# A two-layer decoder trunk: early work on one token half, y's sums moved into layer 0, and another first order in layer 1

## The chip, the core and the metric

The kernel runs on one core of a Trainium2 chip. The metric is the device time of one execution in microseconds. Five engines are spoken of: PE (matrix products), DVE and POOL (elementwise), ACT (activations and copies), SP (which issues DMAs). Each runs its own instructions in a fixed order, set when the program is built; an instruction waits at the head of its queue until its inputs and its buffer are ready.

## The reference

The input x is 1024 tokens by 1024 channels, float32. Two layers follow, each `h = h + mixer(rms_norm(h))`, and a last RMSNorm.

```python
def pooling_mixer(u, w_in, w_group, scale, w_out):        # layer 0
    xb, z = jnp.split(u @ w_in, 2, axis=-1)               # 2048 channels each
    pooled = trailing mean over 2/4/8/16 tokens (4 channel groups) minus self
    mixed = per group of 512 channels: pooled @ w_group[g]
    y = mixed * scale * silu(z)
    return y @ w_out                                      # 2048 -> 1024

def stick_breaking_mixer(u, w_in, w_out):                 # layer 1
    q, k, v, z = split(u @ w_in)                          # 16 heads
    o = stick_breaking_attention(q, k, v)
    return (o * silu(z)) @ w_out
```

## The kernel before, in words

**Products.** A float32 tile is split into a rounded part and a remainder (`split`, lines 92 to 99: a copy on ACT, L97, a subtraction on DVE, L98). `mm3` (lines 86 to 90) makes one product of three matmuls from two split tiles: L88, L89, L90. A tile is 128 x 512.

**Seven products instead of eight.** Layer 0's input projection and output projection use Strassen's scheme in Winograd's form: the operands are cut into 2 x 2 blocks, and seven products of sums of blocks give the four result blocks. For the input projection the blocks of u are named B[j, l, kb]: j is the half of the channels, l the half of the tokens (l = 0 is the later half in memory, `HALVES = (1, 0)`), kb one of four tiles. The operands of the seven products are G[1] to G[7]: G1 and G2 are blocks of the first token half, G3 a block of the second, G4 to G7 sums of blocks of both (`u_sums`, lines 183 to 193).

**Opening** (lines 299 to 314). `load_x(l)` loads eight tiles of x's transpose, squares each on ACT and sums the squares over channels by matmuls against ones (L156), then makes the RMS factor (POOL, L162), spreads it by four transposes (L165) and copies it (L167). `to_u` scales a tile (L173) and splits it into a G. A `Group` is two blocks of 128 output columns; groups at 0 and 2 give xb, those at 16 and 18 z, for the first pooling group. `first` is the product with G1, `second` the one with G2, both into PSUM bank p1; `rest` makes the other five with the weights' sums, which POOL adds (lines 231 to 234 and 257), and DVE combines them. Two groups, `x0` and `x1`, do `first` and `second` on the first token half before the second half is loaded and `u_sums` runs.

**Layer 0's loop** (lines 316 to 332). For each of four pooling groups `gi`: two xb groups, pooling of their four blocks (`pool_block`, DVE), two z groups with SiLU, and for each of four blocks `mixed` (lines 286 to 297): 24 matmuls, the scaling by z on DVE (L295) in the tile t0, and one write of t0, 512 KB, to `y_dram` (L297). There are two buffers for t0, seven for raw weights (`a_raw`).

**Output projection** (lines 347 to 485). Seven products of eight steps each: the first is `ops1`, then `ops6`, one with Y[1, 0], `ops7`, `ops4`, one with S1 and `ops3`. Each step loads weight blocks (`wload`) and, in `ops1` and `ops6`, the four blocks of y (`load_y`, L356). POOL makes the sums of y (L404 to L406, L434) and those of the weights (L410, L411, L430, L470). The x tiles are loaded again and the results added. `to_u1(l)` (lines 449 to 465) makes layer 1's input for a token half: RMS factor, scaling, transposes on PE (L460), split by ACT and DVE (L464, L465). `to_u1(0)` comes before `ops3`, `to_u1(1)` after it.

**Layer 1** (lines 488 to 813). Work comes in items for q and k, z, v and the output projection of a head. PSUM's eight banks go from the pool `banks` to four pools with 3, 2, 2 and 1 banks. `head0` (line 735) is the list of items made before the first scores.

**What sets the order.** The tile framework schedules the instructions of each engine with its own simulation, mostly by program order among those that it takes to be ready; so queues don't follow the text line by line. Tiles of a pool rotate over its buffers, and pools opened later lie in the space of those closed before.

Of the kernel before, what the change touches and what calls it, by code (L numbers as in the profile page):

```python
# [15 lines left out]
P = 128  # L16
# [29 lines left out]
def trunk(ctx, tc, x, xt, g, pw, pg, psc, pwo, sqk, sv, sz, swo, nf, out):  # L46
# [36 lines left out]
    y_dram = dram.tile([DI // P, P, S], F32, name="y_dram")  # L83
# [47 lines left out]
    with tc.tile_pool(name="l0", bufs=2) as l0:  # L131
# [10 lines left out]

        def load_x(l, then={}):
# [22 lines left out]
            rsb = l0.tile([P, 512], F32, name="rsb", bufs=2)  # L166
# [3 lines left out]
        def to_u(k, l, n, rsb):  # L170
# [12 lines left out]
        def u_sums(kb):  # L183
            b11, b21, b12, b22 = B[0, 0, kb], B[1, 0, kb], B[0, 1, kb], B[1, 1, kb]
            t3 = l0.tile([P, 512], F32, name="w_raw", bufs=3)
            nc.vector.tensor_tensor(t3, b22, b12, ALU.subtract)
            u_split(7, kb, t3)
            nc.gpsimd.tensor_tensor(b12, b11, b12, ALU.subtract)
            nc.vector.tensor_tensor(b11, t3, b11, ALU.add)
            u_split(6, kb, b11)  # L190
            u_split(5, kb, b12)
            nc.gpsimd.tensor_tensor(b11, b11, b21, ALU.subtract)
            u_split(4, kb, b11)
# [6 lines left out]
        def tmp():  # L200
            return l0.tile([P, 512], F32, name="avx", bufs=4)

        class Group:


            def __init__(self, c):
                self.c, self.a11, self.a12 = c, None, None

            def load(self):
                self.a11 = raw_of(pw[self.c][:, :512], l0, "a_raw", bufs=7)  # L210

            def first(self):

                if self.a11 is None:
                    self.load()
                self.p1 = bank()
                product(self.p1, split(self.a11), 1)
                self.a1 = tmp()
                act(self.a1, self.p1, AF.Copy)

            def second(self):
                self.a12 = raw_of(pw[self.c][:, 512:], l0, "a_raw", bufs=7)
                product(self.p1, split(self.a12), 2, True)

            def rest(self, dst, fn):

                a11, c = self.a11, self.c
                a21 = raw_of(pw[c + 1][:, :512], l0, "a_raw", bufs=7)
                a22 = raw_of(pw[c + 1][:, 512:], l0, "a_raw", bufs=7)
# [17 lines left out]
                v = tmp()  # L247
                nc.vector.tensor_tensor(v, p6, self.a1, ALU.subtract)
# [5 lines left out]
                if self.a12 is None:  # L254
                    self.second()
                out(0, 0, self.p1, None)
                add(self.a12, self.a12, a11, ALU.add)
                product(p7, split(a22), 4, True)
                out(1, 0, v, p7)
                product(p5, split(self.a12), 3, True)  # L260
# [25 lines left out]
        def mixed(gi, o, pooled, t0):  # L286
# [10 lines left out]
            nc.sync.dma_start(y_dram[kb], t0)  # L297

        x0, x1 = Group(0), Group(2)
        rsb = load_x(0, {1: x0.load, 3: x1.load})  # L300
        for k in range(4):
            to_u(k, 0, 1, rsb)
        x0.first()
        x1.first()
        for k in range(4, 8):
            to_u(k, 0, 2, rsb)
        x0.second()
        x1.second()
        rsb = load_x(1)
        for kb in range(4):  # L310
            to_u(kb, 1, 0, rsb)
            to_u(4 + kb, 1, 3, rsb)
            u_sums(kb)
        nc.sync.dma_start(sc_sb, psc)

        for gi in range(len(WINDOWS)):
            pooled = {}
            for cp in (0, 2):
                grp = (x0 if cp == 0 else x1) if gi == 0 else Group(gi * 4 + cp)
                if gi:  # L320
                    grp.first()
                dst = [xb_tile() for _ in range(2)]
                grp.rest(dst, AF.Copy)
                for i in range(2):
                    pool_block(gi, cp + i, dst[i], pooled)
            for op in (0, 2):
                grp = Group(16 + gi * 4 + op)
                grp.first()
                dst = [l0.tile([P, S], F32, name="t0") for _ in range(2)]
                grp.rest(dst, AF.Silu)  # L330
                for i in range(2):
                    mixed(gi, op + i, pooled, dst[i])
# [14 lines left out]
    with tc.tile_pool(name="ob", bufs=4, reuse_waits="tile") as ob:  # L347
# [3 lines left out]
        Y, T3, S1, S2 = {}, {}, {}, {}  # L351

        def load_y(j, l, kb):
            half = HALVES[l]
            Y[j, l, kb] = slot()
            nc.sync.dma_start(Y[j, l, kb], y_dram[8 * j + kb][:, half * 512:half * 512 + 512])  # L356

        def out_product(ps, operands, more=False, by_tile=None):

            ops = [None] * 8  # L360

            def step(t, kb):
                (wh, wl), (yh, yl) = ops[kb]
                ts_ = slice(t * P, (t + 1) * P)
                mm3(ps[t], yh[:, ts_], yl[:, ts_], wh, wl, kb == 0 and not more, kb == 7, more)

            for kb in range(8):
                ops[kb] = operands(kb)
                for t in range(4):
                    step(t, kb)  # L370
# [17 lines left out]
        def ops1(kb):  # L388
            load_y(0, 0, kb)
# [465 lines left out]
```

## Time and profile before

| | us |
|---|---|
| median of 3 runs (1659.06 to 1661.23) | 1659.06 |
| the profiled execution | 1659.5 |
| its span | 1657.7 |
| PE busy in the span | 1565.2 (94%) |
| DVE busy | 1110.8 (67%) |
| ACT busy | 672.6 (41%) |
| POOL busy | 383.7 (23%) |

The span is the time from the first to the last instruction of the profiled execution; all positions below count from its start. A matmul's end is modelled, so PE's busy time holds overlaps; the distance of two starts is the better price. "Idle" in brackets behind an instruction is what its engine waited just before it, and for whom.

### The profile page before, as it was taken

How to read it: one execution, taken by the hardware profiler on the slowest of the kernel's cores; microseconds unless marked ns; L12 is line 12 of the kernel's file. 1: busy time of each engine (PE TensorE's matmuls, PEld its weight loads, DVE VectorE, ACT ScalarE, POOL GpSimd, SP SyncE). 2: the span in 40 equal slices, each digit the busy share in tenths (PEclk: the TensorE clock that was granted, in tenths of full speed). 3: DMA queues.
4: the chain of work that ended last, by engine and by line, in shares of the span. 5: the costliest groups of instructions: out<-in, count | busy, mean ns of one | idle time of the engine just before them, and what ended most of it. 6: DMA issues, size and time to landing. Idle time of an engine off the chain costs nothing.

```text
span 1657.7 us, 23250 instructions
## 1 busy us (share of the span) xinstructions
PE 1565.2 (94%) x8360; PEld 1349.1 (81%) x8360; DVE 1110.8 (67%) x1643; ACT 672.6 (41%) x1328; POOL 383.7 (23%) x822
## 2 busy tenths in 40 slices
PE   7399999999985999799999999999999999999997
PEld 7278888888863788698988988988988988988986
DVE  3785674957842788457685675676667667657678
ACT  5334232323321445445344434434435435335344
POOL 0542222223029552111111101102102102101113
PEclk9599999999997999899999999999999999999999
DMA  4021221222167450112012011111011011021012
GB/s 146 0 88 67 89 83 70 64 83 64 38 231 264 148 168 3 57 44 59 14 51 65 29 43 57 39 47 49 33 52 52 26 58 45 26 64 39 27 43 104
DMA packets 59955, 113.20 MB, mean 68 GB/s; under 512 B 7360, under 2 KB 7360, under 8 KB 59840
## 3 DMA queue, kind: packets, MB, share of 16 engines
q1 hardware_dynamic: 59696, 111.71, 20.9%
q8 instruction: 66, 1.08, 0.3%
q14 instruction: 49, 0.40, 0.1%
q10 hardware_dynamic: 144, 0.01, 0.0%
HBM read 90.72 MB, written 12.58 MB: 62 GB/s over the span
## 4 chain that ended last, share of the span: by engine, by line
PE 89%; DVE 3%; POOL 3%; DMA 2%; issue 1%; SPq 1%; ACT 1%; POOLq 0%; DVEq 0%; ACTq 0%
PE pd L88 14%; PE pd L90 14%; PE pd L89 14%; PE bk L88 10%; PE bk L89 10%; PE bk L90 10%; PE pt L686 4%; PE po L88 2%; PE po L89 2%; PE po L90 2%; PE pq L642 2%; PE pq L643 2%; DMA slot<-y_dram 2%; PE bk L156 1%; POOL slot L405 0%
## 5 line engine op out<-in xcount | busy, mean ns | idle before, releaser
L654 DVE TENSOR_TENSOR_SCAN om<-om 128x257 f32<-128x257 f32 (+1 forms) x192 | 187.3, 979 | 85.9 <-POOL om L651 34.7
L88 PE MATMUL pd<-slot,w_hi 128*128 128x512 f32 x512 | 202.2, 395 | 8.4 <-DVE slot L465 8.4
L89 PE MATMUL pd<-slot,w_hi 128*128 128x512 f32 x512 | 201.9, 394 | 0.0
L90 PE MATMUL pd<-slot,w_lo 128*128 128x512 f32 x512 | 200.3, 392 | 0.0
L98 DVE TENSOR_TENSOR w_lo<-w_raw,w_hi 128x512 fp32r<-128x512 f32 x192 | 143.4, 756 | 68.6 <-ACT w_hi L97 66.6
L97 ACT ACTIVATE w_hi<-w_raw 128x512 fp32r<-128x512 f32 x192 | 120.0, 630 | 139.9 <-PE pd L89 67.4
L647 ACT ACTIVATE om<-pq 128x256 f32<-128x256 f32 (+1 forms) x192 | 94.4, 492 | 180.1 <-PE pq L643 173.6
L88 PE MATMUL pd<-w_hi,slot 128*128 128x256 f32 x512 | 146.4, 286 | 0.0
L90 PE MATMUL pd<-w_hi,slot 128*128 128x256 f32 x512 | 144.7, 283 | 0.0
L89 PE MATMUL pd<-w_lo,slot 128*128 128x256 f32 x512 | 144.3, 282 | 0.0
L651 POOL TENSOR_SCALAR_AFFINE_SELECT om<-om 128x128 f32<-128x128 f32 x128 | 49.1, 385 | 375.8 <-ACT om L647 373.2
L97 ACT ACTIVATE w_hi<-a_raw 128x512 fp32r<-128x512 f32 x96 | 59.8, 629 | 154.7 <-PE bk L89 108.1
L88 PE MATMUL bk<-w_hi,y_hi 128*128 128x512 f32 x224 | 92.3, 418 | 30.5 <-ACT y_hi L97 22.3
L88 PEld LDWEIGHTS pd<-slot,w_hi 128*128 128x128 f32 x512 | 96.8, 189 | 27.0 <-DVE slot L465 8.7
L690 DVE TENSOR_TENSOR at_l<-pt,at_h 128x512 fp32r<-128x512 f32 (+1 forms) x160 | 99.5, 625 | 20.2 <-ACT at_h L689 20.0
L90 PEld LDWEIGHTS pd<-slot,w_lo 128*128 128x128 f32 x512 | 96.6, 189 | 19.6
L89 PEld LDWEIGHTS pd<-slot,w_hi 128*128 128x128 f32 x512 | 96.6, 189 | 18.7
L689 ACT ACTIVATE at_h<-pt 128x512 fp32r<-128x512 f32 (+1 forms) x160 | 86.6, 552 | 60.5 <-PE pt L686 59.8
L658 DVE TENSOR_TENSOR om<-pq,om 128x256 f32<-128x256 f32 (+1 forms) x192 | 105.0, 551 | 9.2 <-ACT v_h L576 0.5
L88 PE MATMUL pd<-w_hi,y_h 128*128 128x512 f32 x256 | 107.0, 418 | 0.4 <-ACT y_h L715 0.4
L89 PE MATMUL pd<-w_lo,y_h 128*128 128x512 f32 x256 | 102.2, 399 | 0.0
L90 PE MATMUL pd<-w_hi,y_l 128*128 128x512 f32 x256 | 100.3, 395 | 0.0
(182 smaller groups left out, 4031.5 us busy)
## 6 DMA issues: line engine op xcount, KB each, us to landing
w_raw<-in_pwo SPq DMA_DIRECT2D x72, 256.0 KB, 3.9
a_raw<-in_pw SPq DMA_DIRECT2D x64, 256.0 KB, 2.8
y_dram<-t SPq DMA_DIRECT2D x16, 512.0 KB, 2.6
slot<-y_dram SPq DMA_DIRECT2D x32, 256.0 KB, 5.5
w_raw<-in_sqk SPq DMA_DIRECT2D x32, 256.0 KB, 2.8
w_raw<-in_sz SPq DMA_DIRECT2D x32, 256.0 KB, 3.0
w_raw<-in_sv SPq DMA_DIRECT2D x32, 256.0 KB, 2.7
w_raw<-in_swo SPq DMA_DIRECT2D x32, 256.0 KB, 2.6
```

Source lines behind the costliest of these rows:

```text
L88: nc.tensor.matmul(ps, lhsT=lh, rhs=rh, start=start, stop=False, skip_group_check=more)
L89: nc.tensor.matmul(ps, lhsT=lh, rhs=rl, start=False, stop=False, skip_group_check=more)
L90: nc.tensor.matmul(ps, lhsT=ll, rhs=rh, start=False, stop=stop, skip_group_check=more)
L97: act(hi, raw, AF.Copy)
L98: nc.vector.tensor_tensor(lo, raw, hi, ALU.subtract)
L647: act(om[:, 1:1 + n], pz, AF.Sigmoid, scale=-ZSCALE)
L651: nc.gpsimd.affine_select(out=om[:, 1:1 + P], in_=om[:, 1:1 + P], pattern=[[1, P]], base=0, channel_multiplier=-1, compare_op=ALU.is_gt, f ...
L654: nc.vector.tensor_tensor_scan(out=om[:, :1 + n], data0=om[:, :1 + n], data1=om[:, :1 + n], initial=1.0 if s.first else carry[r], op0=ALU. ...
L658: nc.vector.tensor_tensor(om[:, :n], pz, om[:, :n], ALU.mult)
L686: nc.tensor.transpose(tp[:, c * P:(c + 1) * P], om[:, (j - b0) * P:(j - b0 + 1) * P], ident)
L689: act(ah[:, :n], tp[:, :n], AF.Copy)
L690: nc.vector.tensor_tensor(al[:, :n], tp[:, :n], ah[:, :n], ALU.subtract)
```

## The change

The change has four parts. (1) Four groups (two xb, two z) do `first` and `second` on the first token half; they read their a11 and a12 weights again in `rest`. `load_x(1)` adds squares pairwise on POOL before the sum by matmul. `u_sums` scales the second half itself and orders its work by product: G7's and G6's sums first, then the splits of 6, 7, 5, 4, 3. (2) `mixed` makes y's sums on POOL as soon as a block of y is there and writes each of the seven operands to an array of its own in HBM; for the last eight blocks it reads back the matching first two (`old`, one buffer). (3) The output projection loads one y operand per step, and its own y sums are gone. (4) `head0` begins with the later token half of q and z and that half's v; the items for the other half load and split their weights again. Buffers: a_raw 6 instead of 7, avx 5 instead of 4, the RMS factor uses w_raw.

```diff
-    y_dram = dram.tile([DI // P, P, S], F32, name="y_dram")
+    yd = {n: dram.tile([8, P, 512], F32, name=f"y{n}_dram") for n in range(8)}
...
+        def wide(i):
+            return l0.tile([P, S + 16], F32, name="xb" if i % 2 else "wsum")
...
+            def ssq(sq, first, last):
+                for j in range(4):
+                    nc.tensor.matmul(
+                        ps[:, 2 * j:2 * j + 2], lhsT=sq[:, j * P:(j + 1) * P], rhs=ones,
+                        start=first and j == 0, stop=last, skip_group_check=True)
...
-                sq = l0.tile([P, S + 16], F32, name="xb" if k % 2 else "wsum")[:, :512]
+                sq = wide(k)[:, :512]
                 act(sq, t, AF.Square)
-                for j in range(4):
-                    nc.tensor.matmul(
-                        ps[:, 2 * j:2 * j + 2], lhsT=sq[:, j * P:(j + 1) * P], rhs=ones,
-                        start=k == 0 and j == 0, stop=k == NK - 1, skip_group_check=True)
+                if l == 0:
+                    ssq(sq, k == 0, k == NK - 1)
+                elif k % 2:
+                    nc.gpsimd.tensor_tensor(sq, sq, before, ALU.add)
+                    ssq(sq, k == 1, k == NK - 1)
+                before = sq
...
+        def u_sums(rsb):
+            t3 = []
+            for kb in range(4):
+                b11, b12, b22 = B[0, 0, kb], B[0, 1, kb], B[1, 1, kb]
+                to_u(kb, 1, rsb)
+                to_u(4 + kb, 1, rsb)
+                t3.append(wide(kb)[:, :512])
+                nc.vector.tensor_tensor(t3[kb], b22, b12, ALU.subtract)
+                nc.gpsimd.tensor_tensor(b12, b11, b12, ALU.subtract)
+                if kb:
+                    t2(kb - 1, t3)
+            t2(3, t3)
+            for kb in range(4):
+                u_split(7, kb, t3[kb])
+            for kb in range(4):
+                u_split(5, kb, B[0, 1, kb])
+            for kb in range(4):
+                nc.gpsimd.tensor_tensor(B[0, 0, kb], B[0, 0, kb], B[1, 0, kb], ALU.subtract)
+                u_split(4, kb, B[0, 0, kb])
+            for kb in range(4):
+                u_split(3, kb, B[1, 1, kb])
+
+        def t2(kb, t3):
+            nc.vector.tensor_tensor(B[0, 0, kb], t3[kb], B[0, 0, kb], ALU.add)
+            u_split(6, kb, B[0, 0, kb])
...
+            def load(self, i, j):
+                self.a[i, j] = raw_of(pw[self.c + i][:, j * 512:j * 512 + 512], l0, "a_raw", bufs=6)
...
+            def ahead(self):
+                self.second()
+                self.a, self.early = {}, True
...
             def rest(self, dst, fn):
+                if self.early:
+                    self.load(0, 0)
+                else:
+                    self.first()
+                self.load(1, 0)
+                self.load(1, 1)
...
-            nc.sync.dma_start(y_dram[kb], t0)
+            b = t0[:, 512:], t0[:, :512]
+            j, kb = divmod(kb, 8)
+            sub = nc.gpsimd.tensor_tensor
+            def put(n, t):
+                nc.sync.dma_start(yd[n][kb], t)
+            put((1, 2)[j], b[0])
+            put((0, 3)[j], b[1])
+            if j == 0:
+                sub(b[1], b[0], b[1], ALU.subtract)
+                put(5, b[1])
+            else:
+                o = l0.tile([P, S], F32, name="old", bufs=1)
+                for n in range(2):
+                    nc.sync.dma_start(o[:, n * 512:n * 512 + 512], yd[n][kb])
+                b12, b11 = o[:, :512], o[:, 512:]
+                sub(b12, b[1], b12, ALU.subtract)
+                put(7, b12)
+                sub(b11, b12, b11, ALU.add)
+                put(6, b11)
+                sub(b[0], b11, b[0], ALU.subtract)
+                put(4, b[0])
...
+        early = xs + zs
+        rsb = load_x(0, {2 * i + 1: lambda i=i: early[i].load(0, 0) for i in range(4)})
         for k in range(4):
-            to_u(k, 0, 1, rsb)
-        x0.first()
-        x1.first()
+            to_u(k, 0, rsb, 1)
+        for grp in early:
+            grp.first()
         for k in range(4, 8):
-            to_u(k, 0, 2, rsb)
-        x0.second()
-        x1.second()
-        rsb = load_x(1)
-        for kb in range(4):
-            to_u(kb, 1, 0, rsb)
-            to_u(4 + kb, 1, 3, rsb)
-            u_sums(kb)
+            to_u(k, 0, rsb, 2)
+        for grp in early:
+            grp.ahead()
+        u_sums(load_x(1))
...
+        def ysplit(n, kb):
+            return split(raw_of(yd[n][kb], ob, "y_raw"), ob, "y")
...
         def ops6(kb):
-            for jl in ((0, 1), (1, 1), (1, 0)):
-                load_y(*jl, kb)
-            T3[kb] = slot()
-            add(T3[kb], Y[1, 1, kb], Y[0, 1, kb], ALU.subtract)
-            add(Y[0, 1, kb], Y[0, 0, kb], Y[0, 1, kb], ALU.subtract)
-            add(Y[0, 0, kb], T3[kb], Y[0, 0, kb], ALU.add)
             a21, a22, a11 = (wload(*ij, kb) for ij in ((1, 0), (1, 1), (0, 0)))
...
-            return split(S2[kb]), split(Y[0, 0, kb], ob, "y")
+            return split(S2[kb]), ysplit(6, kb)
...
         def ops4(kb):
-            add(Y[0, 0, kb], Y[0, 0, kb], Y[1, 0, kb], ALU.subtract)
-            return split(wload(1, 1, kb)), split(Y[0, 0, kb], ob, "y")
+            return split(wload(1, 1, kb)), ysplit(4, kb)
...
-        head0 = [(("q", 0), qk_item(0)), (("z", 0), z_item(0)), (("v", 0, 1), v_item(0, (3, 2)))]
+        head0 = [(("q", 0, 1), qk_item(0, (1,))), (("z", 0, 1), z_item(0, (1,))), (("v", 0, 1), v_item(0, (3, 2))),
+                 (("q", 0), qk_item(0, (0,))), (("z", 0), z_item(0, (0,)))]
```

## Rows read from the trace of the kernel before

**Rows 1.** The page, part 2: busy tenths of the span's 40 equal slices.
```profile
PE   7399999999985999799999999999999999999997
...
POOL 0542222223029552111111101102102102101113
```

**Rows 2.** PE's timeline, opening: start us, us, engine, line, operation, out<-in, count.
```profile
24.07 1.22 PE L88 MATMUL bk<-g_0h,w_hi 128*128 128x512 f32 x2 [2.13 <-ACT g_0h L180]
...
28.36 1.84 PE L156 MATMUL bk<-ones,wsum 128*128 128x2 f32 x8
...
34.06 0.63 PE L89 MATMUL bk<-g_1l,w_hi 128*128 128x512 f32 x1
...
36.01 0.40 PE L88 MATMUL bk<-g_3h,w_hi 128*128 128x512 f32 x1
...
46.92 1.03 PE L156 MATMUL bk<-ones,xb 128*128 128x2 f32 x8
...
74.42 0.80 PE L88 MATMUL bk<-g_0h,w_hi 128*128 128x512 f32 x1 [24.09 <-ACT w_hi L97]
...
97.59 0.39 PE L88 MATMUL bk<-g_0h,w_hi 128*128 128x512 f32 x1
...
103.04 0.39 PE L88 MATMUL bk<-g_0h,w_hi 128*128 128x512 f32 x1
```

**Rows 3.** Timelines of ACT, DVE and POOL in the opening, same columns.
```profile
50.37 0.60 ACT L167 ACTIVATE rsb<-bk 128x512 f32<-128x512 f32 x1 [6.16 <-PE bk L165]
...
60.52 0.68 DVE L181 TENSOR_TENSOR g_0l<-w_raw,g_0h 128x512 fp32r<-128x512 f32 x1
...
75.39 1.77 DVE L181 TENSOR_TENSOR g_2l<-pl,g_2h 128x512 fp32r<-128x512 f32 x1
...
85.12 0.68 DVE L181 TENSOR_TENSOR g_3l<-pl,g_3h 128x512 fp32r<-128x512 f32 x1
...
57.07 8.15 POOL L188 TENSOR_TENSOR pl<-pl 128x512 f32<-128x512 f32 x3 [7.82 <-DVE w_raw L186]
```

**Rows 4.** Busy time by stretch: us, engines' busy time (count), PEclk, DMA share, GB/s.
```profile
core 0: us, PE busy (x) PEld busy (x) DVE busy (x) ACT busy (x) POOL busy (x), PEclk, DMA share, GB/s
24.07:467.70 443.63, 410.91 (x1796) 339.95 (x1796) 299.86 (x390) 144.66 (x245) 119.08 (x89) 0.96 0.19 62
80.56:97.59 17.03, 12.98 (x42) 10.11 (x43) 12.90 (x17) 4.53 (x9) 12.92 (x8) 0.81 0.25 78
300.00:460.00 160.00, 160.00 (x707) 132.50 (x706) 118.99 (x151) 52.12 (x89) 36.38 (x28) 1.00 0.18 60
500.00:550.00 50.00, 27.69 (x76) 20.57 (x75) 14.44 (x13) 10.63 (x19) 50.00 (x37) 0.73 0.66 220
```

**Rows 5.** PE's and SP's timelines at the turn to the output product.
```profile
467.30 0.39 PE L90 MATMUL bk<-pl,w_lo 128*128 128x512 f32 x1
475.51 2.08 PE L88 MATMUL bk<-w_hi,y_hi 128*128 128x512 f32 x4 [7.82 <-ACT w_hi L97]
...
479.51 0.40 PE L90 MATMUL bk<-w_hi,y_lo 128*128 128x512 f32 x1
...
468.50 0.32 SPq L297 DMA_DIRECT2D y_dram<-t  x1
468.91 0.38 SPq L356 DMA_DIRECT2D slot<-y_dram  x1
```

**Rows 6.** POOL's costliest groups from 467 to 700 us: busy us, mean ns.
```profile
L410 POOL TENSOR_TENSOR s<-w_raw 128x512 f32<-128x512 f32 x8 | 12.0, 1501 | 0.0
```

**Rows 7.** SP's waits, 90 to 470 us: us in total, times, longest us.
```profile
SPq L103 <- DVE w_lo L98: 186.7, 44, 13.6
```

**Rows 8.** The page, part 6: DMA issues, KB each, us to landing.
```profile
a_raw<-in_pw SPq DMA_DIRECT2D x64, 256.0 KB, 2.8
y_dram<-t SPq DMA_DIRECT2D x16, 512.0 KB, 2.6
slot<-y_dram SPq DMA_DIRECT2D x32, 256.0 KB, 5.5
```

**Rows 9.** DVE's and PE's timelines at the turn to layer 1.
```profile
652.44 2.72 DVE L465 SCALAR_TENSOR_TENSOR slot<-bk,g_sb,slot 128x512 fp32r<-128x512 f32 x4
...
682.97 0.75 DVE L465 SCALAR_TENSOR_TENSOR slot<-bk,g_sb,slot 128x512 fp32r<-128x512 f32 x1
...
683.77 0.80 PE L88 MATMUL pd<-slot,w_hi 128*128 128x512 f32 x1 [8.42 <-DVE slot L465]
```

More of the change, by code (lines that the diff above doesn't have):

```diff
@@ L200, in tmp @@
         def tmp():
-            return l0.tile([P, 512], F32, name="avx", bufs=4)
+            return l0.tile([P, 512], F32, name="avx", bufs=5)
         class Group:
             def __init__(self, c):
-                self.c, self.a11, self.a12 = c, None, None
-            def load(self):
-                self.a11 = raw_of(pw[self.c][:, :512], l0, "a_raw", bufs=7)
+                self.c, self.a, self.early = c, {}, False
+            def load(self, i, j):
+                self.a[i, j] = raw_of(pw[self.c + i][:, j * 512:j * 512 + 512], l0, "a_raw", bufs=6)
             def first(self):
-                if self.a11 is None:
-                    self.load()
+                if (0, 0) not in self.a:
+                    self.load(0, 0)
                 self.p1 = bank()
-                product(self.p1, split(self.a11), 1)
+                product(self.p1, split(self.a[0, 0]), 1)
                 self.a1 = tmp()
@@ L253, in rest @@
                 out(1, 1, x_, p5)
-                if self.a12 is None:
+                if self.early:
+                    self.load(0, 1)
+                else:
                     self.second()
                 out(0, 0, self.p1, None)
-                add(self.a12, self.a12, a11, ALU.add)
+                a12 = self.a[0, 1]
+                add(a12, a12, a11, ALU.add)
                 product(p7, split(a22), 4, True)
                 out(1, 0, v, p7)
-                product(p5, split(self.a12), 3, True)
+                product(p5, split(a12), 3, True)
                 out(0, 1, p5, v)
@@ L349, in wload, with out_product @@
             return raw_of(pwo[8 * j + kb][:, i * 512:i * 512 + 512], ob, bufs=6)
[L351 to L365, printed above, removed]
+        S1, S2 = {}, {}
+        def ysplit(n, kb):
+            return split(raw_of(yd[n][kb], ob, "y_raw"), ob, "y")
+        def out_product(ps, operands, more=False):
             for kb in range(8):
-                ops[kb] = operands(kb)
+                (wh, wl), (yh, yl) = operands(kb)
                 for t in range(4):
-                    step(t, kb)
+                    ts_ = slice(t * P, (t + 1) * P)
+                    mm3(ps[t], yh[:, ts_], yl[:, ts_], wh, wl, kb == 0 and not more, kb == 7, more)
         def tmp2(name):
@@ L388, in ops1 @@
         def ops1(kb):
-            load_y(0, 0, kb)
-            return split(wload(0, 0, kb)), split(Y[0, 0, kb], ob, "y")
+            return split(wload(0, 0, kb)), ysplit(1, kb)
         pa = [bank() for _ in range(4)]
@@ L419, in trunk @@
         v = a1
-        out_product(pa, lambda kb: (split(wload(0, 1, kb)), split(Y[1, 0, kb], ob, "y")), True)
+        out_product(pa, lambda kb: (split(wload(0, 1, kb)), ysplit(2, kb)), True)
         for i, t in enumerate(rows(0)):
@@ L470, in ops3 @@
             add(S2[kb], S2[kb], a12, ALU.add)
[L471 removed]
+            return split(S2[kb]), ysplit(3, kb)
         pd = [bank() for _ in range(4)]
[L474 removed]
+        out_product(pd, lambda kb: (split(S1[kb]), ysplit(5, kb)))
         for i, t in enumerate(rows(1)):
@@ L510, in trunk, with qk_item @@
         qk, vt, gt, yt = {}, {}, {}, {}
-        def qk_item(head):
+        def qk_item(head, halves=(1, 0)):
             w2 = load_w(sqk[head])
             yield
-            for half in (1, 0):
+            for half in halves:
                 ps = ps_d.tile([P, 512], F32, name="pd")
@@ L536, in qk_item, with z_item @@
                 yield
-        def z_item(head):
+        def z_item(head, halves=(1, 0)):
             w2 = load_w(sz[head])
             yield
-            for half in (1, 0):
+            for half in halves:
                 ps = ps_d.tile([P, 512], F32, name="pd")
```

57 lines of the change are left out of this document (21 added, 36 removed).

## The prediction, made before the result was known

> **What bounds it now.** I read the page's slices first [rows 1]: PE is busy nearly everywhere and has two dents, one in the opening (slices 2 to 4) and one around slices 12 to 14, where POOL stands at 9 and 5. So the question in each dent is what PE waits for; elsewhere PE sets the time. Then PE's own timeline gives the price of a matmul: a product of twelve takes 103.04 - 97.59 = 5.45 us for two, 0.227 us each [rows 2]. With that price a stretch can be checked against its count.
>
> From the first product at 24.07 to the last matmul of layer 0, 443.6 us, PE ran 1796 matmuls [rows 4]: 1728 of 512 columns (16 groups of 7 x 12, 16 blocks of 24), 393.1 us; 64 of `load_x(1)` at 1.03/8 = 0.13 us, 8.2 us; 4 turns, 0.5 us. So 42 us were lost there, all before 97.6. Reading the opening in order: up to about 36 us matmuls stand 0.43 us apart (0.63 us long), then 0.23 apart [rows 2], the lower and the higher of the clock's two levels (1.2 and 2.4 GHz), after PE had begun in earnest at 24. Then PE runs out of work: the second half's factor is ready at 50.37 [rows 3], and the next product starts at 74.42 after 24.09 us of waiting [rows 2]. Meanwhile DVE makes the sums and low parts; beside POOL one takes 1.77 us rather than 0.68, and three subtractions of POOL take 8.15 us [rows 3].
>
> The second dent: from 500 to 550 PE ran 76 matmuls, 17.3 us of work, so 32.7 us were lost; POOL was busy for all 50.00 us with 37 instructions, the granted clock was 0.73 [rows 4]. POOL is the bound: the six adds of an `ops6` step at about 1.5 us [rows 6] make 9 us where PE's twelve matmuls of that step need 2.7 us.
>
> Between the layers' stages lie two pauses. PE's last matmul of layer 0 starts at 467.30, the next at 475.51, and the higher clock is back by 479.5; SP issues the first load of y only at 468.91 [rows 5]. The first matmul of layer 1 starts at 683.77, after 8.42 us idle behind the last of DVE's L465 [rows 9].
>
> **The change, part by part.** *Opening.* Four groups instead of two run their first two products early: 96 matmuls, 21.8 us, where 48 ran. `load_x(1)` adds its squares in pairs on POOL, so 32 matmuls of 64 fall away: -4.1 us of PE, at four POOL adds that start beside the loads. From 24.07 PE has 21.8 + 4.1 + 0.5 = 26.4 us of work, plus 5.9 us for running 11.8 us at the lower clock as now: it lasts until 56.4. The other side is the chain to the sixth product. The 32 sums fit into the time when DVE still makes the low parts (eight take 1.84 us there [rows 2], 7.4 us, to about 32), and the factor comes some 4 us later at the earliest, 36. If they sit behind first products it is 46, nearer to now. I take 41. Then `u_sums` now puts first what the sixth product needs: 8 scalings, 4 + 4 sums, 4 low parts, 20 DVE instructions: 13 us at 0.64; with POOL beside eight of them 21 us; now, with all 36 instructions mixed, from 50.37 to 85.8 at the latest, 35 us [rows 3]. I take 20, nearest to the case with POOL beside: 61. Lost: 5.9 us (slow start) + 4.7 us (56.4 to 61) + 2.0 us (a slow restart: after the pause that ends at 475.51 nine matmuls take 4.0 us [rows 5]) + 7.5 us, since DVE and POOL still make the other operands as they do today between 80.56 and 97.59, where 42 matmuls took 17.0 us [rows 4]. That is 20.1 us instead of 42, and 4.1 us less work: -26 us. Bounds: -37 (factor at 36, nothing idle, 3 us in the last term) and -5 (46 plus today's 34).
>
> *The early groups' cost.* Eight weight tiles are read twice, 0.26 MB each, in a stretch where DMA is 19% busy [rows 4]: nothing, covered by the weight buffers. These are 6 instead of 7; SP already waits 44 times for one to come free [rows 7], so loads still go out a group ahead of use and land in 2.8 us [rows 8]: nothing. If that lead were gone, each late weight would cost PE up to 2.8 us.
>
> *y's sums in layer 0.* In the first two pooling groups one POOL subtraction and 3 writes per block, in the last two 3 subtractions, 2 reads and 5 writes: 32 POOL instructions at 1.5 us and 80 more DMA issues on SP, less 16. PE covers all that is not late. DVE pays where POOL runs beside it: 24 x 1.07 us = 26 us in the last two groups, to set against 119 us busy of 160 [rows 4]; it stays under 160. What queues behind: a POOL subtraction waits for the block's scaling and for the one buffer `old`, and behind it on POOL stand the next group's weight adds; behind a waiting write on SP stand the next weights; the two t0 tiles come free only after the last write. A block's chain is a read (3 to 5.5 us), three subtractions (4.5), a write (2.6) [rows 6, 8], 10 to 13 us, against 10.9 us (four products) between a pair of blocks and the next use of its t0 tiles. Bounds 0 and +30 (ten us at three hand-overs); I take +3, nearest to the fully busy PE of [rows 4].
>
> The Trainium skill's page "SBUF — State Buffer" (section "Who interferes with whom") says that a VectorE instruction with two SBUF inputs and a GpSimd instruction that reads SBUF block each other for the whole instruction. The trace agrees (1.77 us against 0.68, [rows 3]). Read strictly, it speaks against moving the subtractions to a stretch where DVE is fuller: were two DVE instructions held by each, the 119 us would become some 163 of 160, and the sum would be 1615.
>
> *Turn to the output product.* Today the loads of the new stage follow layer 0's last write in SP's order, [rows 5], though nothing of kb 0 depends on it. If the order stays so, they now follow the last block's three subtractions as well: 8.2 us idle plus 4.3. If they go ahead of it, the pause of 8 us goes. Bounds -8 and +9; I take +4, as the order in the trace has it.
>
> *Output product.* POOL keeps 2 adds of 6 per `ops6` step; 16 adds at 1.5 us, 24 us, can start with the first product and have 43.7 us of PE work beside them. y is now one load per product and tile: 24 more loads, 144 of 0.26 MB; at the 220 GB/s of [rows 4] an `ops6` step with its four loads takes 4.8 us, but the first product's 16 loads leave time to run ahead. I keep 5 us of the 32.7: -28. Bounds -33 and -16 (if eight steps are paced at 4.8 instead of 2.7).
>
> *Order at layer 1.* The later half's q and z come first, and 4 weight tiles are loaded and split again (4 x 1.3 us on ACT and DVE, beside matmuls). But the first matmul already belongs to the later half, whose inputs were made by 655 us [rows 9], and still waits for the last L465; L465 also reads the PSUM banks that this matmul's tile reuses, so I read the wait as one for a bank, and that stays. Take 0; bounds -8 (the pause) and +1.
>
> **Sum.** -26 + 3 + 4 - 28 + 0 = -47 against the profiled execution's 1659.5 us (span 1657.7 and 1.8 around it), 0.4 above the median 1659.06: **1612 us**.
>
> **Rivals.** *All covered:* the factor comes at 36 and the new stage's loads go ahead of the last writes: -37 instead of -26, -8 instead of +4, 1589 us. For it: `load_x(1)` depends on no product. Against: today its last eight matmuls run at 46.92, behind the early products [rows 2]. *Opening not covered:* sums late, operands mixed again, -5 there: 1633 us. *Output product still held,* by loads or DVE: POOL leaves, the steps run at 4.8 us and its adds slow DVE in the first product too: 1612 + 10 to 18, about 1628. *Slower: SP's queue in the last two pooling groups.* `old` has one buffer, so eight chains of about 11.5 us run one after another, and weights behind them in SP's order come late by 11.5 - 5.5 us per block, 48 us, plus 2 us of lower clock after each pause, 16: 1673 us. It decides when the hold outlasts the lead of six weight buffers, about 28 us at four loads per group of 19 us; that speaks against it. *No effect of the new order at layer 1* is inside the forecast.
>
> **How the numbers follow.** Chances: forecast 0.40, all covered 0.22, opening not covered 0.18, output product held 0.11, several small stalls that eat the gain 0.03, SP's queue 0.06. Faster by over 0.2% (3.3 us, about what a measurement of this kernel can tell) 0.91, within it 0.03, slower 0.06. The range 1584 to 1640 reaches from the covered case, with some of layer 1's pause gone, to the uncovered opening with a stall more.
>
> **What would show it.** Opening: no idle of 24 us before a first matmul on the sixth product, the factor's copy (L167's successor) before 46; wrong if PE still idles over 15 us. Output product: POOL under half busy, PE's count full from its first tile on. Turn: PE idle 10 to 15 us; under 4 would show the covered case. Layer 1: first matmul still behind the last L465. Between 100 and 460 PE idle beyond 10 us in all, ended by POOL or by a late weight, would make the queue rival right.

## The result, and the profile after

The changed kernel takes 1623.5 us (median of 4 runs, 1622.17 to 1624.09), the kernel before 1659.9 beside it: ratio 0.9779, 95% interval 0.9762 to 0.9796. The forecast was 1612 us in a range of 1584 to 1640. The profiled execution took 1624.09 us, its span 1622.4.

The two profiles are laid side by side at five points of PE's timeline (us from the span's start; in brackets what PE idled just before):

| | before | after | difference |
|---|---|---|---|
| second half's factor copied (ACT) | 50.37 | 56.12 | +5.75 |
| first matmul on sums of blocks | 74.42 (24.09) | 81.57 (25.48) | +7.15 |
| last matmul of layer 0 | 467.30 | 457.26 | -10.0 |
| first matmul of the output product | 475.51 (7.82) | 471.96 (14.31) | -3.5 |
| last matmul of the output product | 667.04 | 635.59 | -31.4 |
| first matmul of layer 1 | 683.77 (8.42) | 647.93 (4.03) | -35.8 |

By stage: opening and steady part -10.0, turn +6.5, output product -27.9, entry into layer 1 -4.4; behind that both kernels take the same time to half a microsecond (the spans differ by 35.3).

The slices of the page answer to [rows 1]: the dent in slices 12 and 13 has become one slice at 6, the opening still has its dent in slice 2, and POOL's 9 is gone. The granted clock (PEclk) stands at 7 tenths in slices 2 and 12 alone, where PE pauses.

```profile
PE   7399999999969998999999999999999999999997
...
POOL 2562233254235252011102101101101102101113
PEclk9799999999979999999999999999999999999999
```

PE's timeline of the opening after the change, beside [rows 2] (start us, us, engine, line, operation, count, idle before and releaser):

```profile
52.67 0.40 PE L91 MATMUL bk<-g_3h,w_lo 128*128 128x512 f32 x1
52.90 1.18 PE L155 MATMUL bk<-ones,xb 128*128 128x2 f32 x10
55.44 0.65 PE L178 MATMUL bk<-ident,rs 128*128 128x128 f32 x4 [1.36 <-POOL rs L175]
81.57 1.22 PE L89 MATMUL bk<-g_0h,w_hi 128*128 128x512 f32 x2 [25.48 <-ACT g_0h L193]
```

The last ten sums for the second half's factor (L155) run at 52.90, directly behind the last of the eight early products. So the factor waits for all of them, and PE has no product left to run when it comes. ACT, DVE and POOL then, beside [rows 3], in the same columns:

```profile
56.12 0.60 ACT L180 ACTIVATE w_raw<-bk 128x512 f32<-128x512 f32 x1 [13.99 <-PE bk L178]
...
56.75 8.40 DVE L186 SCALAR_TENSOR_TENSOR pl<-pl,g_sb,w_raw 128x512 f32<-128x512 f32 x8 [2.48 <-ACT w_raw L180]
...
72.30 0.68 DVE L194 TENSOR_TENSOR g_3l<-pl,g_3h 128x512 fp32r<-128x512 f32 x1
74.13 1.74 DVE L220 TENSOR_TENSOR pl<-wsum,pl 128x512 f32<-128x512 f32 x1 [1.16 <-POOL pl L205]
75.80 1.75 DVE L194 TENSOR_TENSOR g_0l<-wsum,g_0h 128x512 fp32r<-128x512 f32 x1
...
65.83 11.16 POOL L205 TENSOR_TENSOR pl<-pl 128x512 f32<-128x512 f32 x3 [4.54 <-DVE wsum L204]
```

From the factor to the first product on sums it is 25.45 us. In it DVE runs eight scalings (L186, 8.40 us), thirteen instructions of 0.68 us, and, after a wait for POOL, four of 1.75 us. POOL's three subtractions (L205) take 11.16 us, for DVE runs on at 0.68 beside them.

Busy time by stretch, beside [rows 4] (columns as there):

```profile
60.00:80.00 20.00, 0.00 (x0) 0.00 (x0) 18.84 (x24) 8.87 (x16) 15.46 (x6) 0.50 0.17 54
100.00:440.00 340.00, 339.01 (x1493) 279.61 (x1492) 252.31 (x319) 112.02 (x191) 120.25 (x92) 1.00 0.29 96
471.96:635.98 164.02, 161.61 (x704) 132.28 (x704) 122.14 (x154) 77.63 (x141) 65.00 (x52) 0.97 0.70 231
500.00:550.00 50.00, 47.59 (x201) 38.01 (x200) 40.34 (x46) 22.68 (x39) 23.39 (x18) 0.97 0.84 281
```

In the steady part PE has no gap to speak of although POOL works 120 us of 340. From 500 to 550 PE runs 201 matmuls where it ran 76, and POOL is busy for 23.39 us instead of all 50.

The turn, beside [rows 5]: SP's queue, then POOL, ACT and PE.

```profile
458.46 0.79 SPq L341 DMA_DIRECT2D y_dram<-t  x2
459.54 0.82 SPq L351 DMA_DIRECT2D old<-y_dram  x2
463.68 1.66 SPq L341 DMA_DIRECT2D y_dram<-old  x2
466.36 0.32 SPq L341 DMA_DIRECT2D y_dram<-t  x1
466.73 0.42 SPq L104 DMA_DIRECT2D w_raw<-in_pwo  x1
...
462.40 1.26 POOL L353 TENSOR_TENSOR old<-t,old 128x512 f32<-128x512 f32 x1 [3.58 <-DMA old<-y_dram]
...
465.07 1.26 POOL L357 TENSOR_TENSOR t<-old,t 128x512 f32<-128x512 f32 x1
...
470.53 0.63 ACT L98 ACTIVATE w_hi<-w_raw 128x512 fp32r<-128x512 f32 x1 [16.63 <-DMA w_raw<-in_pwo]
...
457.26 0.39 PE L91 MATMUL bk<-pl,w_lo 128*128 128x512 f32 x1
471.96 2.07 PE L89 MATMUL bk<-w_hi,y_hi 128*128 128x512 f32 x4 [14.31 <-ACT y_hi L98]
```

The last block's chain is a read (`old`, for which POOL waits 3.58 us), three subtractions and three writes. Only then SP issues the first load of output weights (466.73), which ACT can split at 470.53.

DVE and PE at the entry into layer 1, beside [rows 9]:

```profile
647.13 0.74 DVE L506 SCALAR_TENSOR_TENSOR slot<-bk,g_sb,slot 128x512 fp32r<-128x512 f32 x1
...
651.51 0.74 DVE L506 SCALAR_TENSOR_TENSOR slot<-bk,g_sb,slot 128x512 fp32r<-128x512 f32 x1
...
635.59 0.39 PE L91 MATMUL bk<-w_hi,y_lo 128*128 128x512 f32 x1
...
647.93 0.50 PE L89 MATMUL pd<-slot,w_hi 128*128 128x512 f32 x1 [4.03 <-DVE slot L506]
```

Before, the last matmul of the output product stood here:

```profile
667.04 0.39 PE L90 MATMUL bk<-w_hi,y_lo 128*128 128x512 f32 x1
```

After the change layer 1's first matmul starts 0.06 us behind the end of the fifth of the eight L506 (647.13 is the fifth, 651.51 the last). Before, it followed the last of L465.

### The profile page after: what moved, and what is told of

The parts are those of the page before. It is cut to its first block, busy times and chain, and to the rows that moved or that the text cites. A ratio compares the mean times of both kernels' runs of the same rounds, so it can differ in the third digit from the quotient of the medians.

```text
span 1622.4 us, 23428 instructions
## 1 busy us (share of the span) xinstructions
PE 1552.7 (96%) x8328; PEld 1336.8 (82%) x8328; DVE 1120.4 (69%) x1647; ACT 674.0 (42%) x1332; POOL 399.6 (25%) x826
## 3 DMA queue, kind: packets, MB, share of 16 engines
q1 hardware_dynamic: 74096, 133.74, 25.4%
## 4 chain that ended last, share of the span: by engine, by line
PE 88%; DVE 5%; issue 2%; POOL 2%; ACT 1%; DMA 1%; SPq 0%; POOLq 0%; DVEq 0%; ACTq 0%
PE pd L89 15%; PE pd L91 14%; PE pd L90 14%; PE bk L89 10%; PE bk L90 10%; PE bk L91 10%; PE pt L727 4%; PE po L89 2%; PE po L90 2%; PE po L91 2%; PE pq L683 2%; PE pq L684 2%; PE bk L155 1%; DVE pl L186 1%; DVE w_lo L99 1%
## 5 line engine op out<-in xcount | busy, mean ns | idle before, releaser
L99 DVE TENSOR_TENSOR w_lo<-a_raw,w_hi 128x512 fp32r<-128x512 f32 x96 | 75.4, 788 | 39.1 <-ACT w_hi L98 39.1
```

The source lines that it names most:

```text
L99: nc.vector.tensor_tensor(lo, raw, hi, ALU.subtract)
```

## The experiments

### Which part gives what: e1, e2, e3

e1 takes the opening alone; y is one array again, its sums are made in the output projection, and `head0` is that of before:

```diff
-            put((1, 2)[j], b[0])
-            put((0, 3)[j], b[1])
...
+            nc.sync.dma_start(y_dram[kb], t0)
```

> Only the opening of the change (four early groups, paired squares, sums by product); y's sums stay in the output product and layer 1 begins as before. Theory: layer 0's last matmul comes 10 us earlier as in the changed kernel (457 instead of 467), and everything behind it is shifted: 1650 us, ratio 0.994. Rival (the opening only pays off because the stage behind is faster, or the early groups cost later): no gain, 1657 to 1662.

Measured: 1645.15 us, ratio 0.9912 (0.9897 to 0.9927). Layer 0's last matmul comes at 456.72, as the theory had it. The turn (8.3 us) and the output product (191.7) are as before. The entry into layer 1 is 4.4 us shorter, as in the full change; the theory did not have that.

e2 takes y's sums alone, with `load_x`, `u_sums`, the groups and `head0` of before and six weight buffers:

```diff
-                if l == 0:
-                    ssq(sq, k == 0, k == NK - 1)
-                elif k % 2:
-                    nc.gpsimd.tensor_tensor(sq, sq, before, ALU.add)
...
-        def u_sums(rsb):
+        def u_sums(kb):
```

> Only y's sums made in layer 0 and read per product; opening and first order of layer 1 as before. Theory: the turn costs about 6 us more (pause of 14 to 15 us instead of 8) and the output product 26 us less: about 1640 us, ratio 0.988, POOL no longer busy throughout after the turn. Rival (the last 6 us at layer 1 come from the y part too, through the banks): 1634. If the POOL subtractions held up the steady part of layer 0, its last matmul would come later than 467 by more than 2 us.

Measured: 1632.19 us, 0.9836 (0.9819 to 0.9852), the rival's time. Layer 0's last matmul comes at 466.25 (467.30 before), so the sums cost PE nothing there. The turn is 15.1 us, the output product 164.0, and the entry into layer 1 11.2 us instead of 16.7. PE's row of e2 at the entry:

```profile
656.50 0.47 PE L89 MATMUL pd<-slot,w_hi 128*128 128x512 f32 x1 [2.87 <-ACT slot L474]
```

The two gains, 14.8 and 27.7, sum to 42.5 against 36.4 together: the shorter entry appears in both alone and can be had only once.

e3 is the change with `head0` in its old order:

```diff
-        head0 = [(("q", 0, 1), qk_item(0, (1,))), (("z", 0, 1), z_item(0, (1,))), (("v", 0, 1), v_item(0, (3, 2))),
-                 (("q", 0), qk_item(0, (0,))), (("z", 0), z_item(0, (0,)))]
+        head0 = [(("q", 0), qk_item(0)), (("z", 0), z_item(0)), (("v", 0, 1), v_item(0, (3, 2)))]
```

> The changed kernel with layer 1's first order of before (q, z, v, both halves each). Theory: the first matmul of layer 1 waits for a PSUM bank whatever the order, and starts as in the changed kernel about 12 us after the last of the output product: 1623 us, within 2 us. Rival (the new order lets PE begin before the second half's inputs are complete): first matmul back behind the last of the eight L506 instructions, idle 8 us instead of 4, and 1628 to 1630 us.

Measured: 1622.45 us, 0.9775 (0.9761 to 0.979), first matmul of layer 1 with the same 4.04 us of idle before it. The time differs from the changed kernel's by 1 us, well inside the intervals: the new order gives nothing that these runs can tell.

### The opening: early products against the factor (e4, e5, e8, e12)

e4 puts the second half's factor ahead of the second products in program order:

```diff
+        rsb1 = load_x(1)
         for k in range(4, 8):
             to_u(k, 0, rsb, 2)
         for grp in early:
             grp.ahead()
-        u_sums(load_x(1))
+        u_sums(rsb1)
```

> The changed kernel with the second half's load and factor put ahead of the second products of the four early groups in the program, nothing else. Theory: the factor was late only because its last ten matmuls stood behind all eight early products in PE's queue; now it is copied at about 45 instead of 56, the sixth product starts about 25 us later, near 70 instead of 81.6, and the pause before it shrinks from 25.5 to about 15 us: 1612 us. Rival (DVE and POOL are held by other work, so that the operands come no sooner): under 3 us gained.

Measured: 1618.63 us, 0.975 (0.9736 to 0.9765). The factor's copy came at 48.52, after 7.34 us of waiting for its transposes, which still stood behind products in PE's queue; the theory had it at 45. The product on sums came at 70.97 after 17.24 us idle, 22.5 us behind the factor (25.4 in the changed kernel). So the product moved with the factor, and the gain was less than hoped because the factor moved less.

e5 leaves two groups early instead of four:

```diff
-        early = xs + zs
+        early = xs
```

> After the change, but only two groups instead of four do their first products early; the new order of the sums stays. Theory (the opening gained because 10.9 us of PE work, 48 matmuls, were put in front of a pause that kept its length, against a factor 5.7 us later; the order of the sums gave little): the factor near 50, the pause near 25, the last matmul of layer 0 about 5 us later than the changed kernel's 457.3, the time about 1629. Rival (the gain is the new order of the sums): within 2 us of the changed kernel's 1623.5.

Measured: 1619.91 us, 0.9755 (0.9739 to 0.9772). The theory wanted 1629 and the rival a time within 2 us of 1623.5, so neither held. By the times, whose intervals overlap a little, e5 is no slower than the changed kernel; by the trace it is ahead. PE's timeline of e5, then a row of DVE's:

```profile
43.04 0.60 PE L178 MATMUL bk<-ident,rs 128*128 128x128 f32 x4
66.12 1.22 PE L89 MATMUL bk<-g_0h,w_hi 128*128 128x512 f32 x2 [22.48 <-ACT g_0h L193]
452.56 0.39 PE L91 MATMUL bk<-pl,w_lo 128*128 128x512 f32 x1
...
44.31 5.39 DVE L186 SCALAR_TENSOR_TENSOR pl<-pl,g_sb,w_raw 128x512 f32<-128x512 f32 x8 [6.51 <-ACT w_raw L180]
```

Without the two extra groups the factor is copied at 43.68 (56.12 with them), the product on sums starts 15.45 us earlier, and layer 0 ends 4.7 us earlier, though 10.9 us of products are left for later. Of the 15.45 us, 12.4 are the factor: the early products pushed it back by their own length, and a little more. The other 3.0 are the eight scalings, 5.39 us here and in e4 and 8.40 in the changed kernel, where four of POOL's weight adds run beside them (55.35 to 61.28). So four groups instead of two bought nothing in this order.

From the product on sums to the end of layer 0 it is 386.4 us here and 392.9 before. I put these 6.4 us down to the new order of the sums: behind that product PE waits 1.36 and 1.03 us here, and 3.20 and 4.05 us before:

```profile
80.56 0.80 PE L90 MATMUL bk<-g_0h,w_lo 128*128 128x512 f32 x1 [3.20 <-DVE w_lo L98]
...
93.12 0.50 PE L88 MATMUL bk<-g_0h,w_hi 128*128 128x512 f32 x1 [4.05 <-DVE avx L251]
```

No run changes the order alone, and e2, with the old order, has 390.9 us, so about 2 us of it came without the new order. After the change the stretch is 375.7 us, 17.2 less than before: the 10.9 of work done early, and 6.3 more.

e8 puts `load_x(1)` ahead of all early products:

```diff
+        rsb1 = load_x(1)
         for grp in early:
             grp.first()
...
-        u_sums(load_x(1))
+        u_sums(rsb1)
```

> After the change, but load_x(1) stands directly behind load_x(0), ahead of all early products, so the second half's factor can be made while the first products run. Theory (the factor sets the sixth product, 22 to 25 us ahead of it): factor near 40, sixth product near 63 while PE's early work lasts to about 56, pause under 8 us, time about 1611. Rival (the work for the first half comes later by as much, or the operands are bound by DVE and POOL): within 4 us of the 1618.6 that the factor ahead of the second products gave.

Measured: 1611.63 us, 0.9708 (0.9693 to 0.9722). PE's timeline of e8:

```profile
35.60 1.11 PE L178 MATMUL bk<-ident,rs 128*128 128x128 f32 x4 [5.97 <-POOL rs L175]
...
57.28 0.39 PE L90 MATMUL bk<-g_0l,w_hi 128*128 128x512 f32 x1
59.68 0.50 PE L91 MATMUL bk<-g_0h,w_lo 128*128 128x512 f32 x1 [2.01 <-DVE w_lo L99]
...
79.84 0.79 PE L89 MATMUL bk<-g_0h,w_hi 128*128 128x512 f32 x1 [7.42 <-ACT w_hi L98]
```

The factor is there at 36.7, the early products hold PE until 57, and the pause of 25 us is down to 2.0. A wait of 7.4 us near 80 is next. Layer 0 ends at 443.46, 13.8 us earlier than in the changed kernel.

e12 is e8 with e5's edit, two groups (`early = xs`). 

> load_x(1) ahead of all early products, as in e8, but two groups early instead of four: the fourth cell beside the changed kernel (factor behind four groups, 1623.5), e5 (behind two, 1619.9) and e8 (ahead of four, 1611.6). Theory (two more groups are worth their 10.9 us only where the factor doesn't stand behind them): the factor near 37 as in e8, PE's early work ends near 46, a pause of 10 to 13 us before the sixth product near 58, the last matmul of layer 0 some 9 us behind e8's 443.5, the time about 1620. Rival (the operands are bound by DVE and POOL whatever PE holds in front, or the factor is all that counts): within 3 us of 1611.6.

Measured: 1616.49 us, 0.9737 (0.9721 to 0.9754). The early work ends near 50, the pause before the product on sums (59.16) is 8.80 us, layer 0 ends at 449.22. So two groups are slower than four here, as the theory had it, by 5 us where it had 8 to 9; the two intervals touch, but the times themselves don't (1610.7 to 1611.9 for e8, 1615.3 to 1617.3 here). The four cells:

| | two groups early | four groups early |
|---|---|---|
| factor behind the early products | 1619.9 (e5) | 1623.5 (the change) |
| factor ahead of them | 1616.5 (e12) | 1611.6 (e8) |

The two extra groups cost 3.6 us where the factor stands behind them and gain 4.9 where it stands ahead. Up to the end of layer 0 it is 4.7 and 5.8 us. Behind that, with two groups, the turn is some 0.6 us longer and the entry into layer 1 over 1 us shorter in both rows, so the times measure the opening only to about a microsecond.

### POOL and DVE in the sums: e6, e10

e6 moves the four subtractions b11 - b12 of `u_sums` from POOL to DVE:

```diff
-                nc.gpsimd.tensor_tensor(b12, b11, b12, ALU.subtract)
+                nc.vector.tensor_tensor(b12, b11, b12, ALU.subtract)
```

> After the change, but u_sums' four subtractions b11 - b12 run on DVE instead of POOL. Theory (the sixth product comes 25 us after the factor because three of POOL's subtractions stand still for 11.2 us while DVE runs, and DVE's sums, which overwrite what they read, wait for them): the product starts near 73 instead of 81.6, the pause is 17 us instead of 25.5, the time about 1616. Rival (DVE is the bound, and four instructions more on it cost what the wait gave): within 3 us of 1623.5.

Measured: 1622.69 us, 0.9777 (0.9762 to 0.9792), the rival's time. The product on sums starts at 78.39, 3.2 us earlier, and nothing is left of it at the end of layer 0 (457.26 again). POOL's and DVE's timelines of e6 show where the stall went:

```profile
70.28 15.17 POOL L268 TENSOR_TENSOR w_raw<-a_raw 128x512 f32<-128x512 f32 x1 [9.71 <-DMA a_raw<-in_pw]
...
70.37 0.68 DVE L205 TENSOR_TENSOR pl<-pl 128x512 f32<-128x512 f32 x1
...
83.62 0.68 DVE L194 TENSOR_TENSOR g_3l<-pl,g_3h 128x512 fp32r<-128x512 f32 x1
```

A single POOL add takes 15.17 us. It ends 1.15 us after the last of 23 DVE instructions that ran back to back. It makes a sum of weights, and behind it PE waits 3.6 us for splits of weights (at 88.89, 93.71 and 96.42), which takes back what the earlier product gave.

e10 stands on e9 (below) and moves G4's four subtractions to DVE instead:

```diff
-                nc.gpsimd.tensor_tensor(B[0, 0, kb], B[0, 0, kb], B[1, 0, kb], ALU.subtract)
+                nc.vector.tensor_tensor(B[0, 0, kb], B[0, 0, kb], B[1, 0, kb], ALU.subtract)
```

> As the run with POOL's queue, but the four subtractions for G4 (b11 - b21) run on DVE instead of POOL. Theory (the one long wait left in the opening, 7.4 us near 80, is for weight sums of the next group that stand on POOL behind these subtractions): the wait shrinks by 3 to 5 us and the time by as much. Rival (as with the other four subtractions, POOL's next instruction then stands still while DVE runs on): within 2 us.

Measured: 1608.69 us, 0.9688 (0.9672 to 0.9704). The wait near 80 shrank from 7.38 to 4.38 us, as the theory had it. But the time is within 2 us of e9's, as the rival had it: the ratio lies within the interval of e9, and the four runs spread from 1606.29 to 1611.74 us, so no gain is shown.

### The turn: e7, e9

e7 sends the last block's writes and reads on ACT's DMA queue:

```diff
+            queue = nc.scalar if (gi, o) == (3, 3) else nc.sync
...
-                nc.sync.dma_start(yd[n][kb], t)
+                queue.dma_start(yd[n][kb], t)
```

> After the change, but the last block's five writes and two reads of y go out on ACT's DMA queue instead of SP's. Theory (SP's queue, in order, holds the new stage's first loads behind the last block's chain): the first load of output weights is issued near 459 instead of 466.7, the pause of 14.3 us shrinks to about 8, the time is about 1617.5. Rival (the loads wait for buffers that lie in layer 0's space): pause and time stay, within 1.5 us of 1623.5.

Measured: 1621.53 us, 0.9769 (0.9755 to 0.9784), no gain outside the intervals; the pause is 12.23 us instead of 14.31. SP's and ACT's rows of e7:

```profile
458.27 0.33 SPq L104 DMA_DIRECT2D w_raw<-in_pwo  x1
...
464.29 1.67 ACTq L343 DMA_DIRECT2D y_dram<-old  x2
466.97 0.33 ACTq L343 DMA_DIRECT2D y_dram<-t  x1
467.39 0.63 ACT L98 ACTIVATE w_hi<-w_raw 128x512 fp32r<-128x512 f32 x1 [14.79 <-DMA y_dram<-old]
```

The load left 8.5 us earlier, as the theory said. But the writes now stand in ACT's own order, and the first split (467.39) waits behind the last of them (466.97) instead: the chain had only changed its queue.

e9 stands on e8 and takes POOL's queue (`nc.gpsimd` in place of `nc.scalar`, otherwise e7's edit). 

> The factor first, as in the run before, and the last block's five writes and two reads of y go out on POOL's DMA queue, where nothing of the new stage's first steps waits behind them. Theory (the last block's chain holds the new stage only through the queue that its transfers share with the loads, SP's, or with the splits, ACT's): first load of output weights issued within 2 us of the last matmul of layer 0, splits 3 to 4 us later, the pause 5 to 8 us instead of 14.5, the time about 1604. Rival (the first loads wait for space of layer 0 or for the chain's transfers): pause over 11 us, time 1609 to 1612.

Measured: 1610.4 us, 0.9698 (0.9684 to 0.9713). SP's and PE's rows of e9:

```profile
447.52 0.32 SPq L343 DMA_DIRECT2D y_dram<-t  x1
447.94 0.38 SPq L104 DMA_DIRECT2D w_raw<-in_pwo  x1
...
454.46 2.08 PE L89 MATMUL bk<-w_hi,y_hi 128*128 128x512 f32 x4 [9.91 <-ACT y_hi L98]
```

The pause is 9.91 us instead of e8's 14.49: between the two expectations, since the last write of the block before still stands on SP (447.52) ahead of the load. The output product starts 3.9 us earlier than in e8 and layer 1 2.6 us earlier; the time differs from e8's by less than the intervals. e9 and e10 are the fastest versions run, about 13 to 15 us below the changed kernel.

### The entry into layer 1: e11

e11 adds five transposes into banks that nobody reads:

```diff
+            for _ in range(5 if l else 0):
+                nc.tensor.transpose(bank()[:, :P], ident, ident)
             for k in range(NK):
                 tp = bank()
```

> The changed kernel with five transposes more, into banks that nobody reads, ahead of the last to_u1's eight. Theory (layer 1's first matmul waits for the PSUM bank that its tile reuses, and which of the eight copies held it is the place in the rotation: the last before the change, the fifth after): the rotation moves on by five, the first matmul waits for the last copy again, L508 near 651.5, idle before it 7 to 9 us instead of 4.0, the time 3 to 5 us more, about 1627. Rival (the entry is shorter because of other work or order): idle stays 4.0, time within 1.5 us of 1623.5.

Measured: 1627.06 us, 0.9798 (0.9782 to 0.9815). PE's and DVE's rows of e11:

```profile
649.82 0.74 DVE L508 SCALAR_TENSOR_TENSOR slot<-bk,g_sb,slot 128x512 fp32r<-128x512 f32 x1
...
650.62 0.80 PE L89 MATMUL pd<-slot,w_hi 128*128 128x512 f32 x1 [7.16 <-DVE slot L508]
```

The wait moved from the fifth to the seventh of the eight (not to the last), the idle from 4.03 to 7.16 us, the time by 3.6. No work of layer 1 was touched, so the wait is for a bank and its length depends on which copy held that bank. What decides this is open. The theory's count of banks gave the eighth copy and the seventh came; and e6, which allocates the same banks as the changed kernel and only moves four subtractions to another engine, has a shorter wait, ended by ACT's fifth copy:

```profile
645.32 0.47 PE L89 MATMUL pd<-slot,w_hi 128*128 128x512 f32 x1 [2.87 <-ACT slot L505]
```

## Why the prediction was right and where it was wrong

**Total.** -47 was forecast and -36 came; the sign and the range were right. The two big terms stood on different ground: the output product was read from rows and came out to 0.1 us (the 5 us that it kept as lost were a choice, and that this choice fitted so closely is luck); the opening rested on a choice between bounds and failed. That the total missed by no more than 11.5 us is luck too, for 4.4 us came from a shorter entry into layer 1 that was not forecast.

**Opening, -26 forecast; with the steady part -23 against -10.0.** The step that failed is "If they sit behind first products it is 46, nearer to now. I take 41." The factor came at 56.1, outside my own bounds, since the sums sat behind all eight early products, not only the first ones. I had the row that warned of it: before the change, too, the last eight sums ran behind the early products. I cited it for a rival and still priced the change as if only the amount of early work changed, not its place ahead of the sums. e5 and e8 settle it: taking early products away brought the factor forward, and with the factor ahead of them the pause was 2.0 us. The second failed size is "I take 20" for the way from factor to product: it was 25.4, and 22.5 in e4 and e5. It counted 20 DVE instructions, and DVE ran 25 before that product; the scalings it priced at 0.64 us each, and beside POOL's weight adds they took 1.05. Of the 20.6 us by which that product missed the forecast of 61, 15.1 are the factor and 5.4 the operands. A little came back: I kept 7.5 us of lost time between the products behind it, and 6.3 us of such time went, as far as e5 tells through the new order of the sums. The rival "opening not covered" had this mechanism; its other half, operands mixed again, did not come. The lower bound there is also summed wrong: by the forecast's own terms it is about -7 rather than -5, and nothing hangs on it.

**Steady part, +3.** PE ran 339.0 of 340 us between 100 and 440, and in e2 layer 0 ended no later than before: about nothing, within the bounds. The slower case, SP's queue, did not show; PE's waits in that stretch sum to 1.9 us. The price for DVE was too high: e2, which moves y's sums alone, shows it in the same stretch (before, then e2):

```profile
100.00:440.00 340.00, 340.00 (x1502) 281.53 (x1501) 234.97 (x307) 113.01 (x191) 83.08 (x67) 1.00 0.21 71
100.00:440.00 340.00, 340.00 (x1502) 281.53 (x1501) 243.69 (x308) 113.10 (x193) 114.85 (x88) 1.00 0.28 93
```

POOL has 31.8 us more work, and DVE is busy for 8.7 us more, where the forecast had 26 in the last two groups alone. Read strictly, the rule of the Trainium skill ("SBUF — State Buffer", "Who interferes with whom") would have filled DVE there; with 243.7 of 340 us, 72%, it is far from full. Here the measurement decides.

**Turn, +4, bounds -8 and +9.** +6.5: the order was as read, the last block's chain ahead of the first load; the term was 2.5 us too small. The 4.3 us that it added were the three subtractions, without the read ahead of them, for which POOL waited 3.58 us. e7 and e9 show the queue as the cause of the pause: with the chain on another queue the first load left 8.5 us earlier than in the changed kernel and 5.3 us earlier than in e8, and the pause shrank to 12.2 and 9.9 us. In the time neither gains more than the intervals.

**Output product, -28.** -27.9. POOL was the bound, and with its sums made earlier PE's own count sets the time: 161.6 of 164.0 us.

**Layer 1, 0.** The order gave 0 (e3), and the wait for a bank stayed (e11). The forecast's "that stays" failed for the length of the wait: the bank that the first tile takes was held by the fifth copy rather than the eighth, and the entry was 4.4 us shorter. It is a side effect of the other parts of the change, for e1 and e2 have it too; what in them moves it is not shown.

**Sum of the errors.** 13.0 (opening and steady) + 2.5 (turn) + 0.1 - 4.4 = 11.2 us, of the 11.5 between 1612 and 1623.5.

## What to carry to other kernels

Work put into a pause helps only if it doesn't stand, on the same engine, ahead of the chain that ends the pause: price early work by its place in the queue against the small instructions that others wait for, and issue those first. When a stage ends with a chain of dependent transfers, look at every queue that the next stage's first loads and splits share with it; moving the chain to another queue shortened the pause most where the next stage's first loads and splits did not stand there (e9 against e7). A stall between DVE and POOL need not go when an instruction moves from POOL to DVE: in e6 POOL's next one inherited it.

## What the runs showed of the hardware that was not expected

I had expected that beside POOL each DVE instruction slows to about 1.77 us. The traces show two behaviours of a row of DVE instructions beside POOL, both with their inputs in SBUF. In one, POOL stands until DVE pauses: three subtractions took 11.16 us after the change, and a single add took 15.17 us in e6 (alone it takes 1.26), with DVE at its 0.68 throughout. In the other the two go in turn, DVE 1.75 and POOL about 1.7 us each; after the change this begins when DVE has waited 1.16 us for POOL (74.13).

What decides between the two is not shown. In e8 the two go in turn from 51.55, and later a POOL subtraction stands again beside DVE at 0.68:

```profile
65.13 5.29 POOL L214 TENSOR_TENSOR pl<-pl 128x512 f32<-128x512 f32 x1 [1.88 <-DVE g_0l L194]
```

And in the kernel before, POOL's subtraction at 73.27 got its turn (1.65 us, DVE's next instruction 1.76) though the profile shows no wait of DVE just ahead of it.

The page "SBUF — State Buffer" of the Trainium skill (section "Who interferes with whom") says that the order of issue decides who blocks whom, for a whole instruction. The turns agree with it. The other behaviour does not, if the starts in the profile are the order of issue: the add of e6 starts at 70.28, ahead of the 23 DVE instructions that start from 70.37 to 83.62, and each of them ran first.
